# A hybrid decoder layer on one core: the order of the first gathered blocks, and of ScalarE's copies behind them

## The chip, the core and the metric

The kernel runs on one core of one Trainium2 chip. The metric is the time of one execution on the device, in microseconds (us). A core has five engines that matter here, each with its own queue of instructions, worked in order: TensorE (PE in the profile, with its weight loads as PEld), VectorE (DVE), ScalarE (ACT), GpSimd (POOL) and SyncE (SP). They meet through semaphores. TensorE writes its results into PSUM, which has eight banks; VectorE and ScalarE copy them out into SBUF.

## The reference, cut to what matters

One decoder layer over 256 tokens of width 2048: two groups of attention heads, an output projection and a layer norm; then PEER, a retrieval of single-neuron experts; then a gated embedding. All three norms are over alpha times the residual plus the new part. The change lies in PEER:

```python
q = (xt @ wq).reshape(t, PEER_HEADS, PEER_QDIM)
sa = jnp.einsum('thc,nc->thn', qa, sub_keys[0])
sb = jnp.einsum('thc,nc->thn', qb, sub_keys[1])
va, ia = lax.top_k(sa, PEER_TOPK)
vb, ib = lax.top_k(sb, PEER_TOPK)
top, sel = lax.top_k(cand, PEER_TOPK)            # cand: all sums va + vb
eidx = jnp.take_along_axis(cidx, sel, axis=-1)   # cidx = ia * 128 + ib
gates = jax.nn.softmax(top, axis=-1)
act = jax.nn.gelu(jnp.einsum('thed,td->the', u[eidx], xb))
out = jnp.einsum('the,thed->td', gates * act, v[eidx])
```

Each token picks, in each of 8 heads, 16 of 16384 experts. An expert has a row of u and a row of v, 2048 numbers each. A token's dot product with the u row goes through gelu, is weighted by the gate, and multiplies the v row.

## The kernel before, in words

**Stages.** In order of time: the attention projections and heads, the output projection and first norm, the PEER queries and scores with the top-16 searches on VectorE, the sorting of the experts, the u blocks, the v blocks, the second norm, the gated embedding and the third norm.

**Which experts are gathered.** The last 224 tokens form seven groups of 32 ("units" 1 to 7; the first 32 tokens go another way, row by row, through `sparse_work`). `flags` counts with products of one-hot matrices which experts each unit uses. `classes` sorts the experts by the set of units that use them: one unit (singles), two (pairs), three that lie on a "line", four that form a "quad", and the rest. There are 42 such classes and the rest; each is a 128 x 128 matrix of flags in `I`. `classes` is a generator: its first half makes the seven quads (K4 to KR), its second, at the second `next(sorting)`, everything else (K1 to K4). A class has a fixed number of slots, and 128 slots of the same units make a block. There are 101 blocks; `U_ORDER` is the order in which they are worked: the first six quad blocks, then quads, lines, strips (pairs) and singles mixed, then the rest mixed with the remaining singles. A block is "wide" where its units lie at even steps, so that one product takes all of them; the first nine quad blocks are all wide, with four units each.

**From flags to row numbers.** For a class, `offsets(k0, k1)` (L1029) counts the flags of each column with one product a class, copies the counts (`cs`), sums them over the columns before with one more product, and copies that (`off`). `running(k0, n, tag, on_act)` (L1046) makes running counts of up to four classes, two 128-wide products a class, and copies them out on ScalarE or VectorE. `list_marks`, `list_rows` and `list_index` then find for three blocks at a time the row number of each slot (`idx`). `lists(i1)` is a generator over these up to block i1, and `list_work` runs `lists(6)`, then the ten `running` calls over all classes but quads and the rest, then `lists` for the others, then more. A step of it is run either directly (`run(listing, 1)`), or by `fetch_u` when a block's row numbers are still missing, or by `pace`: this takes a number of microseconds and runs, for each of them, 0.9 steps of the side work that is next (the gates, the lists, then the placing of the gates in `W`), and a share of the gathers for the first 32 tokens.

**A u block.** `fetch_u` (L1437) issues the indirect gather of 128 rows of u on GpSimd into one of five slots. `turn(i, c)` (L1444), for c from 0 to 3, transposes 128 x 512 of block i with four TensorE products (L1451) into one of three PSUM banks with tag T, and copies that to `uT` on ScalarE (L1453). `u_products` (L1455) makes the dot products: for a wide block sixteen products that have `uT` as their weights (L1459; the trace shows each as two instructions), with a `pace` after every second one; for the others products of 32 tokens at a time, that lay the units beside one another in the bank (L1474). Results go to one of two PSUM banks with tag U; `running` uses these tags, too. `u_out` (L1502) brings the result into the order of `W`: for a wide block with a gelu from the bank (L1539 or L1523), for another block first with transposes or products on TensorE from `part`, a copy of the bank (L1658), and then with a gelu. Where the gate already stands in `W`, the gelu goes to `acts`, and `weigh` multiplies it into `W` on VectorE later.

**The order around the change** is written out by hand: `keep` keeps each engine's instructions in the order of the program. Before the loop over the blocks stand five gathers, the four turns of block 0, the second half of the sorting, `offsets(0, K4)`, one list step and two steps of the gates. In the loop, block i + 1 is turned ahead of the products of block i. In the first pass, a list step follows the first two turns of block 1 in the place of a pace. Behind the products of block i stands on ScalarE either the gelu of a wide block, or the copy `part` of another one, whose `u_out` comes after the last turn of the next pass.

**The v blocks** follow: 101 gathers of 128 rows of v and products with `W` into seven banks (L1686). Up to thirteen rows' slots can be filled ahead; the first four gathers start once the placing is done.

Of the kernel before, what the change touches and what calls it, by code (L numbers as in the profile page):

```python
# [10 lines left out]
F32 = mybir.dt.float32  # L11
# [9 lines left out]
P = 128  # L21
# [52 lines left out]
K4 = K3 + len(LINES)  # L74
KR = K4 + len(QUADS)
NK = KR + 1
# [84 lines left out]
START, BLOCKS, NC = _blocks()  # L161


def _mix(*lists):

    todo = [(j + 0.5) / len(x) for x in lists for j in range(len(x))]
    flat = [b for x in lists for b in x]
    return [flat[i] for i in sorted(range(len(flat)), key=lambda i: todo[i])]
# [1 line left out]

NEARLY = 14
SINGLES = [BLOCKS["single"][6 * g + k] for k in range(6) for g in range(NG)]
U_ORDER = (BLOCKS["quad"][:6] + _mix(BLOCKS["quad"][6:], BLOCKS["line"], BLOCKS["strip"],
                                     SINGLES[:NEARLY])
           + _mix(BLOCKS["rest"], SINGLES[NEARLY:]))
NB = len(U_ORDER)
# [117 lines left out]
def build(tc, a, out):  # L294
    nc = tc.nc
# [490 lines left out]
    keep = tc.keep_in_program_order  # L786
# [242 lines left out]
    def offsets(k0, k1):  # L1029

        ps = pbank(pu, "ps_off", "G", 2)
        for k in range(k0, k1):
            keep(nc.tensor.matmul(ps[:, k:k + 1], I[:, k, 2:], ones16[:, :1], start=True,
                                  stop=True))
        keep(nc.vector.tensor_copy(cs[:, k0:k1], ps[:, k0:k1]))
        keep(nc.tensor.matmul(ps[:, 64:64 + k1 - k0], ahead, cs[:, k0:k1], start=True, stop=True))
        if k1 == NK:
            keep(nc.tensor.matmul(ps[:, 128:129], ones16, cs[:, KR:NK], start=True, stop=True))
        keep(nc.vector.tensor_copy(off[:, k0:k1], ps[:, 64:64 + k1 - k0]))
        if k1 == NK:  # L1040
            keep(nc.vector.tensor_scalar(total, ps[:, 128:129], -float(CAPR), 0.0, op0=ALU.add,
                                         op1=ALU.max))
            keep(nc.vector.tensor_scalar(okc, ps[:, 128:129], float(CAPR), 1.0 / GSCALE,
                                         op0=ALU.is_le, op1=ALU.mult))
# [44 lines left out]
    def lists(i1):  # L1089

        nonlocal listed
        made = []
        for i0 in range(listed, i1, 3):
            n = min(3, i1 - i0)
            es = [list_marks(i) for i in range(i0, i0 + n)]
            made.append((i0, n, list_rows(i0, es)))
            yield
            if len(made) > 1:
                i, m, ps = made.pop(0)
                list_index(i, m, ps)  # L1100
                listed = i + m
                yield
        while made:
            i, m, ps = made.pop(0)
            list_index(i, m, ps)
            listed = i + m
            yield
# [33 lines left out]

    def list_work():

        yield from lists(6)
        for i, (k0, n) in enumerate([x for r in ((K3, K4), (K2, K3), (K1, K2))
                                     for x in spread(*r)]):
            running(k0, n, "TU"[i % 2], i % 3 < 2)
            if i % 3 == 2:
                yield
        yield from lists(UPOS[id(BLOCKS["rest"][0])])  # L1150
        for lo, hi in ((K1, K2), (K2, K3), (K3, K4), (K4, KR)):
            for k0, n in spread(lo, hi):
                yield from places_of(k0, n)
        yield
        keep(nc.vector.scalar_tensor_tensor(I[:, KR, 2:], posf, 0.0, some, op0=ALU.is_equal,
                                            op1=ALU.mult))
        offsets(KR, NK)
        yield
        running(KR, 1, "G", True)
        yield  # L1160
        yield from places_of(KR, 1)
        pu32 = lp.tile([P, P], U32, name="pu32")
        keep(nc.vector.tensor_copy(pu32, posf))
        keep(nc.vector.tensor_scalar(pu32, pu32, 13, 0x38000000, op0=ALU.logical_shift_left,
                                     op1=ALU.bitwise_or))
        keep(nc.vector.tensor_copy(map16, pu32.bitcast(F32)))
        yield
        yield from lists(NB)
# [189 lines left out]
    def run(work, n):  # L1358

        for _ in range(n):  # L1360
            if next(work, "end") == "end":
                return True
        return False
# [52 lines left out]
    pools.close("hotp")  # L1416
    sorting = classes(flp, cnt, I, some)
    next(sorting)
    offsets(K4, KR)
    for i, (k0, n) in enumerate(spread(K4, KR)):  # L1420
        running(k0, n, "TU"[i], i == 0)

    listing, gating, sparse, placing = list_work(), gates(), sparse_work(), None
# [20 lines left out]
    def turn(i, c):  # L1444
        if i >= NB:
            return
        if not c:
            turned[i] = ulp.tile([P, D], F32, name="uT", tag="uT", bufs=2)
        ps = pbank(pu, "ps_T", "T", 3)
        for j in range(4):  # L1450
            keep(nc.tensor.transpose(ps[:, j * P:(j + 1) * P],  # L1451
                                     rows[i][:, (4 * c + j) * P:(4 * c + j + 1) * P], ident))
        keep(nc.scalar.copy(turned[i][:, c * 512:(c + 1) * 512], ps))  # L1453
# [46 lines left out]
    late = []  # L1500
# [113 lines left out]
    def weigh(n):  # L1614
        while len(late) > n:
            dst, x = late.pop(0)
            keep(nc.vector.tensor_tensor(dst, dst, x, op=ALU.mult))
# [3 lines left out]
    def pace(us):  # L1621
        side(us)
        gathers(us * grate)
# [1 line left out]
    for _ in range(WF):  # L1625
        fetch_u()
    ulp = pools.open("ulp", "left", bufs=1)
    for c in range(4):
        turn(0, c)
    next(sorting)  # L1630
    offsets(0, K4)
    pools.close("flp")
    run(listing, 1)
    run(gating, 2)
    pending = None
    for i, block in enumerate(U_ORDER):
        grate = GRATES[i >= UPOS[id(BLOCKS["rest"][0])]]
        fetch_u()
        old = len(late)
        for c in range(4):  # L1640
            turn(i + 1, c)
            if c == 3 and pending:
                u_out(*pending)
                pending = None
            if i or c > 1:
                pace(block.quarter)
            else:
                run(listing, 1)
            if c == 1:
                weigh(len(late) - old)  # L1650
        ps = pbank(pu, "ps_u", "U", 2)
        u_products(block, ps, turned.pop(i))
        if block.wide:
            u_out(block, ps)
        else:
            n = P * len(block.windows)
            part = ulp.tile([P, 512], F32, name="part", tag="part", bufs=2)
            keep(nc.scalar.copy(part[:, :n], ps[:, :n]))  # L1658
            pending = block, part
        held = max(min(NB - 2 - i, WF), 0)  # L1660
        if i >= NB - LEAD - NVX - 1 and places_done:
            fetch_v(0)
    if pending:
        u_out(*pending)
    weigh(0)
    assert places_done
    pools.close("ulp", "pu")
# [321 lines left out]
    ps = ln2_T(0, 0, 2)  # L1989
# [17 lines left out]
    ps = ln2_T(1, 0, 4)  # L2007
# [8 lines left out]
    ps = ln2_T(1, 4, 4)  # L2016
# [191 lines left out]
```

## Time and profile before

| what | value |
|---|---|
| time, median of 3 runs | 1519.4 us (1517.67 to 1522.47) |
| the profiled execution's own time | 1515.78 us |
| its span, first to last instruction | 1513.7 us |
| mean granted TensorE clock | 0.97 |
| TensorE busy | 1405.3 us, 93% of the span |
| VectorE, ScalarE, GpSimd busy | 892.4, 634.0 and 430.9 us |
| DMA, mean over the span | 266 GB/s, 402.79 MB |
| first transposes of a u block | at 599.0 us |
| last transposes of a u block | at 1138.9 us |

Lines are those of the kernel before. In a group or a timeline row, `ps_T<-ident,uf` means that `ps_T` is written from `ident` and `uf`, `x16` that sixteen such instructions are taken together, and the part in brackets or behind the last bar is idle time of the engine before them with what ended it. TensorE's products are pipelined and their ends are modelled. A clock of 1.00 is full speed.

### The profile page before, as it was taken

The page shows a single profiled execution, that of the slowest core. Times are in us where ns is not written, and L with a number is a line of the kernel's source. Part 1 is how long each engine was busy: PE and PEld are TensorE (multiplying, and loading weights), DVE is VectorE, ACT ScalarE, POOL GpSimd, SP SyncE. Part 2 cuts the span into 40 slices and gives each one's busy share as a digit, 9 for nine tenths or more (in the row PEclk, how much of TensorE's full clock was granted, in tenths as well). Part 3 has the DMA queues.
Part 4 walks back from the last instruction along what each step waited for, and adds up shares of the span by engine and source line. Part 5 has one row for each costly group of instructions (what it writes and reads, how often), then busy time and mean ns, then how long its engine had stood idle before and what let it go on. Part 6 is the DMA issues. An engine that isn't in the chain of part 4 may idle for free.

```text
span 1513.7 us, 32441 instructions
## 1 busy us (share of the span) xinstructions
PE 1405.3 (93%) x13184; PEld 1092.3 (72%) x13184; DVE 892.4 (59%) x2487; ACT 634.0 (42%) x1311; POOL 430.9 (28%) x386
## 2 busy tenths in 40 slices
PE   9999999999999945999999899988999999995898
PEld 7888888887888834997888888888885333331686
DVE  5455568976559996679756676778532000005767
ACT  5578547875411154444544454444451000003632
POOL 0033213310120021243443343442554444421000
PEclk9999999999999966999999999999999999997899
DMA  8655665558544102788899888899999999999471
GB/s 305 198 167 167 204 201 153 149 161 317 185 153 150 30 30 110 289 297 322 301 353 344 297 325 309 320 394 362 376 383 396 420 418 418 414 385 347 170 267 56
DMA packets 74587, 402.79 MB, mean 266 GB/s; under 512 B 10836, under 2 KB 12916, under 8 KB 36436
## 3 DMA queue, kind: packets, MB, share of 16 engines
q0 software_dynamic: 39280, 272.11, 46.2%
q1 hardware_dynamic: 33424, 125.41, 24.8%
q10 hardware_dynamic: 1728, 3.15, 0.6%
q8 instruction: 104, 1.70, 0.4%
q14 instruction: 51, 0.42, 0.1%
HBM read 404.97 MB, written 4.45 MB: 270 GB/s over the span
## 4 chain that ended last, share of the span: by engine, by line
PE 69%; DMA 10%; issue 8%; DVE 5%; ACT 4%; POOL 3%; POOLq 0%; another core or an unknown queue 0%; ACTq 0%; DVEq 0%
PE ps_T L1451 12%; PE ps_u L1474 8%; PE ps_qk L333 8%; PE ps_q L345 7%; PE ps_u L1459 7%; PE ps_qk L335 4%; DMA vf<-v_rows,idx 4%; DMA vx<-v_rows,idx 3%; PE ps_v L352 2%; PE ps_v L353 2%; PE ps_v L354 2%; PE ps_gate L352 2%; PE ps_gate L353 2%; PE ps_gate L354 2%; PE ps_mix L353 1%
## 5 line engine op out<-in xcount | busy, mean ns | idle before, releaser
L236 DVE TENSOR_TENSOR wl<-wf,wh 128x1024 fp32r<-128x1024 f32 (+1 forms) x167 | 193.0, 1170 | 102.9 <-ACT wh L235 101.6
L1451 PE MATMUL ps_T<-ident,uf 128*128 128x128 f32 x1616 | 220.7, 279 | 26.2 <-ACT uT L1453 17.7
L1453 ACT COPY uT<-ps_T 128x512 f32<-128x512 f32 x404 | 213.6, 598 | 36.5 <-PE ps_T L1451 32.6
L1426 POOL DMA_INDIRECT uf<-u_rows,idx x101 | 132.2, 1309 | 316.2 <-PE ps_T L1451 136.1
L1451 PEld LDWEIGHTS ps_T<-ident,uf 128*128 128x128 f32 x1616 | 176.1, 142 | 50.7 <-ACT uT L1453 25.3
L235 ACT CAST wh<-wf 128x1024 fp32r<-128x1024 f32 (+1 forms) x167 | 155.0, 945 | 114.2 <-PE ps_v L354 30.3
L333 PE MATMUL ps_qk<-X,wh 128*128 128x512 f32 x512 | 185.2, 401 | 0.0
L335 PE MATMUL ps_qk<-X,wl 128*128 128x256 f32 x512 | 145.7, 285 | 0.0
L1474 PE MATMUL ps_u<-uT,XF 128*32 128x128 f32 x3904 | 136.8, 275 | 7.4 <-issue 7.2
L1459 PE MATMUL ps_u<-XF,uT 128*128 128x128 f32 (+2 forms) x832 | 132.5, 311 | 0.0
L1733 DVE BATCH_NORM_STATS2 st<-ps_v 128x6 f32<-128x512 f32 x8 | 5.6, 700 | 213.6 <-PE ps_v L1769 160.5
L1686 PE MATMUL ps_v<-vf,W 128*32 128x512 f32 x936 | 112.0, 612 | 18.2 <-DMA vf<-v_rows,idx 18.2
L1474 PEld LDWEIGHTS ps_u<-uT,XF 128*32 128x32 f32 x3904 | 105.5, 109 | 25.1 <-issue 20.8
L1459 PEld LDWEIGHTS ps_u<-XF,uT 128*128 128x128 f32 x832 | 119.9, 192 | 0.3
L345 PE MATMUL ps_q<-XF,wf 128*128 128x256 f32 x512 | 113.5, 379 | 0.0
L333 PEld LDWEIGHTS ps_qk<-X,wh 128*128 128x128 f32 x512 | 96.4, 188 | 22.0 <-issue 1.0
L1201 DVE SCALAR_TENSOR_TENSOR junk<-io,ibF,ps_find 128x128 f16<-128x128 f16 x224 | 64.5, 344 | 75.7 <-PE ps_find L1193 65.0
L345 PEld LDWEIGHTS ps_q<-XF,wf 128*128 128x128 f32 x512 | 95.9, 190 | 12.3
L1331 DVE SCALAR_TENSOR_TENSOR y<-gb,ew,y 128x2048 f32<-128x2048 f32 x31 | 72.8, 2348 | 47.3 <-DMA gb<-v_rows,eig 47.3
L1686 PEld LDWEIGHTS ps_v<-vf,W 128*32 128x32 f32 x936 | 32.7, 111 | 91.1 <-issue 68.9
L335 PEld LDWEIGHTS ps_qk<-X,wl 128*128 128x128 f32 x512 | 96.3, 188 | 2.5 <-issue 1.3
L1658 ACT COPY part<-ps_u 128x128 f32<-128x128 f32 (+1 forms) x75 | 22.1, 295 | 144.0 <-PE ps_u L1474 85.9
(357 smaller groups left out, 2512.6 us busy)
## 6 DMA issues: line engine op xcount, KB each, us to landing
wf<-w_qk SPq DMA_DIRECT2D x64, 512.0 KB, 3.6
wf<-w_out SPq DMA_DIRECT2D x32, 512.0 KB, 3.6
wf<-peer_wq SPq DMA_DIRECT2D x16, 1024.0 KB, 5.2
wf<-ple_gate SPq DMA_DIRECT2D x16, 1024.0 KB, 9.8
wf<-w_v SPq DMA_DIRECT2D x16, 512.0 KB, 4.1
wf<-w_sv SPq DMA_DIRECT2D x15, 512.0 KB, 6.0
iarow<-s_iar SPq DMA_DIRECT2D x14, 512.0 KB, 8.8
x<-x SPq DMA_DIRECT2D x2, 1024.0 KB, 5.8
```

Of the source, the lines that this page charges most:

```text
L235: self.order(nc.scalar.copy(wh, src))
L236: self.order(nc.vector.tensor_tensor(wl, src, wh.bitcast(F32), op=ALU.subtract))
L333: nc.tensor.matmul(ps, wh[:, j * P:(j + 1) * P], xt[:, dt, :], start=dt == 0, stop=False)
L335: nc.tensor.matmul(ps[:, :T], wl[:, j * P:(j + 1) * P], xt[:, dt, :T], start=False, stop=dt == ND - 1)
L345: nc.tensor.matmul(ps[:, :T - t0], wf[:, dt * P:(dt + 1) * P], xt[:, dt, t0:], start=dt == 0, stop=dt == ND - 1)
L353: order(nc.tensor.matmul(ps, hi, wl, start=False, stop=False))
L1426: keep(nc.gpsimd.indirect_dma_start(out=dst, out_offset=None, in_=src, in_offset=bass.IndirectOffsetOnAxis(ap=idx[:, col:col + 1], axis=0) ...
L1451: keep(nc.tensor.transpose(ps[:, j * P:(j + 1) * P], rows[i][:, (4 * c + j) * P:(4 * c + j + 1) * P], ident))
L1453: keep(nc.scalar.copy(turned[i][:, c * 512:(c + 1) * 512], ps))
L1459: keep(nc.tensor.matmul(ps[:, :n], uT[:, d * P:(d + 1) * P], groups_of(d, *block.wide), start=d == 0, stop=d == ND - 1))
L1474: keep(nc.tensor.matmul(ps[32 * q:32 * q + 32, w * P:(w + 1) * P], XF[:, d, t0:t0 + 32], uT[:, d * P:(d + 1) * P], start=first and not w, ...
L1686: keep(nc.tensor.matmul(ps[32 * j:32 * j + 32], w, vf[:, j * 512:(j + 1) * 512], start=False, stop=last))
```

## The change

Four things are changed. The first nine quad blocks, not six, stand at the front of `U_ORDER`, and `list_work` lists them before its running counts. `offsets` becomes a generator that pauses between its counts and the rest; for the classes of the second half of the sorting, the sorting and the counts are put ahead of the first turn of block 0, and the rest of `offsets` between the first turn and the other three. The three direct list steps are gone. In the first pass, the products of block 0 come first and block 1 is turned behind them, with a pace after each of its four turns. And in all passes, the bank of block i - 1 is taken care of between the turns of block i + 1: the copy `part` of a block that is not wide behind the first turn, and `u_out`, with the gelu of a wide block too, behind the fourth.

```diff
+NFIRST = 9
+U_ORDER = (BLOCKS["quad"][:NFIRST] + _mix(BLOCKS["quad"][NFIRST:], BLOCKS["line"], BLOCKS["strip"],
...
         keep(nc.vector.tensor_copy(cs[:, k0:k1], ps[:, k0:k1]))
+        yield
...
-        yield from lists(6)
+        yield from lists(NFIRST)
...
-        offsets(KR, NK)
+        list(offsets(KR, NK))
...
-    offsets(K4, KR)
+    list(offsets(K4, KR))
...
-    for c in range(4):
+    next(sorting)
+    placed = offsets(0, K4)
+    next(placed)
+    turn(0, 0)
+    list(placed)
+    for c in range(1, 4):
         turn(0, c)
-    next(sorting)
-    offsets(0, K4)
     pools.close("flp")
-    run(listing, 1)
     run(gating, 2)
-    pending = None
+    behind = []
+
+    def parts_out(block, ps):
+        if block.wide:
+            return block, ps
+        n = P * len(block.windows)
+        part = ulp.tile([P, 512], F32, name="part", tag="part", bufs=2)
+        keep(nc.scalar.copy(part[:, :n], ps[:, :n]))
+        return block, part
+
+    def next_turned(i):
+        old = len(late)
+        for c in range(4):
+            turn(i + 1, c)
+            if c == 0 and behind:
+                behind[0] = parts_out(*behind[0])
+            if c == 3 and behind:
+                u_out(*behind.pop())
+            pace(U_ORDER[i].quarter)
+            if c == 1:
+                weigh(len(late) - old)
+
     for i, block in enumerate(U_ORDER):
         grate = GRATES[i >= UPOS[id(BLOCKS["rest"][0])]]
         fetch_u()
-        old = len(late)
-        for c in range(4):
-            turn(i + 1, c)
-            if c == 3 and pending:
-                u_out(*pending)
-                pending = None
-            if i or c > 1:
-                pace(block.quarter)
-            else:
-                run(listing, 1)
-            if c == 1:
-                weigh(len(late) - old)
+        if i:
+            next_turned(i)
         ps = pbank(pu, "ps_u", "U", 2)
         u_products(block, ps, turned.pop(i))
-        if block.wide:
-            u_out(block, ps)
-        else:
-            n = P * len(block.windows)
-            part = ulp.tile([P, 512], F32, name="part", tag="part", bufs=2)
-            keep(nc.scalar.copy(part[:, :n], ps[:, :n]))
-            pending = block, part
+        if not i:
+            next_turned(i)
+        behind.append((block, ps))
...
-    if pending:
-        u_out(*pending)
+    u_out(*parts_out(*behind.pop()))
```

More of the change, by code (lines that the diff above doesn't have):

```diff
@@ L172 @@
 SINGLES = [BLOCKS["single"][6 * g + k] for k in range(6) for g in range(NG)]
-U_ORDER = (BLOCKS["quad"][:6] + _mix(BLOCKS["quad"][6:], BLOCKS["line"], BLOCKS["strip"],
+NFIRST = 9
+U_ORDER = (BLOCKS["quad"][:NFIRST] + _mix(BLOCKS["quad"][NFIRST:], BLOCKS["line"], BLOCKS["strip"],
                                      SINGLES[:NEARLY])
```

## The prediction, made before the changed kernel was run

> **What bounds the kernel now.** I read the page's slices first, then TensorE's timeline where the changed code begins, then the clock there, then the waits of the long stage behind it.
>
> ```profile
> span 1513.7 us, 32441 instructions
> ...
> PE   9999999999999945999999899988999999995898
> ```
>
> TensorE is busy nearly everywhere. The deep dip (slices 14 and 15, 530 to 605 us) is the passage from the scores to the u rows. The change starts at the end of that dip. TensorE there (start, length, idle time before and what ended it):
>
> ```profile
> 599.00 3.57 PE L1451 MATMUL ps_T<-ident,uf 128*128 128x128 f32 x16 [7.23 <-DMA uf<-u_rows,idx]
> 602.40 1.02 PE L1033 MATMUL ps_off<-ones,I 128*128 128x1 f16 x35
> 604.51 0.18 PE L1036 MATMUL ps_off<-cs,ahead 128*128 128x35 f16 x1 [1.09 <-DVE cs L1035]
> ...
> 618.45 0.66 PE L1451 MATMUL ps_T<-ident,uf 128*128 128x128 f32 x4 [0.68 <-ACT uT L1453]
> 618.95 3.29 PE L1459 MATMUL ps_u<-XF,uT 128*128 128x128 f32 x28
> ...
> 622.74 1.99 PE L1451 MATMUL ps_T<-ident,uf 128*128 128x128 f32 x16
> ```
>
> TensorE waits 7.23 us for the first gathered rows, turns them, does the 35 column counts, waits 1.09 us for their copy, and stands 0.68 us at 618.45. At 618.95 begin the second block's products; I use that as the landmark, since everything before it is the same work in both kernels. The granted clock in three stretches (columns: length; busy time of PE, PEld, DVE, ACT, POOL; clock; DMA share; GB/s):
>
> ```profile
> 598.90:602.30 3.40, 3.30 (x16) 3.30 (x17) 0.00 (x0) 1.61 (x3) 0.79 (x1) 0.50 0.99 414
> 602.30:605.70 3.40, 2.31 (x59) 2.23 (x58) 0.39 (x2) 1.25 (x4) 0.99 (x1) 1.00 1.01 426
> 605.70:609.10 3.40, 3.40 (x32) 3.34 (x30) 1.02 (x2) 2.35 (x6) 0.00 (x0) 0.51 1.01 426
> ```
>
> It rises to 1.00 after a busy stretch of 3.4 us and falls back to 0.5 after the stretch that holds the counts and the 1.09 us wait.
>
> From 640 to 1140 us TensorE's stage is the u blocks. Its waits there (total, times, longest), the largest kind:
>
> ```profile
> PE ps_T L1451 <- ACT uT L1453: 17.0, 22, 2.4
> ```
>
> Behind that the v rows run gapless on TensorE:
>
> ```profile
> L1686 PE MATMUL ps_v<-vf,W 128*32 128x512 f32 x891 | 101.5, 592 | 0.0
> L1686 PE MATMUL ps_v<-vx,W 128*32 128x512 f32 x662 | 77.1, 592 | 0.5 <-issue 0.5
> ```
>
> **The change part by part.** *Counts into the gather's shadow.* The sorting's second half, the 35 counts and the copy now come ahead of the second to fourth transpose groups. VectorE before:
>
> ```profile
> 590.37 1.06 DVE L1063 TENSOR_SCALAR mark<-io,off 128x128 f16<-128x128 f16 x6
> ...
> 597.45 0.19 DVE L1009 TENSOR_SCALAR some<-wh 128x128 f16<-128x128 f16 x1
> 604.26 0.20 DVE L1035 CAST cs<-ps_off 128x35 f16<-128x35 f32 x1 [6.63 <-PE ps_off L1033]
> ```
>
> With nine blocks listed ahead instead of six, one list step of three marks more stands before the third index: 3 x 1.06/6 = 0.53 us. Sorting then ends near 597.45 + 0.53 = 598.0, the counts near 599.1, about 0.15 us after the rows land at 599.0. So of the counts' 1.02 us some 0.85 is gained, and the 1.09 us wait goes whole, as the copy (0.20 us) lies under the first transpose group (3.57/4 = 0.9 us). Without the shadow, if sorting came 2 us later, the counts would cost what they do now. Bounds of both together: 0.9 to 2.1; I take 1.94.
>
> *Clock.* With the counts gone from 602.3 to 605.7 and dense products there instead, the stretch at 0.51 should run at 1.00: half of 3.4 us, 1.7. Bounds 0 and 1.7. The row shows sixteen transposes alone (x16, then 1.00) lifting the clock. The Trainium skill, "TensorE: Matmul & The Clock Gate", section "Part 4: PE-mode transpose", says that transposes do not count as busy; by that, 598.9 to 602.3 would not have lifted it, the gain would be 0 and the sum 4.1. The row decides against it. The same page's section "Part 1: The HAM clock gate" has the window free-running, which would make this gain a matter of chance; that is a rival below.
>
> *Table load.* The first gelu stands today between the products and the copies that the next transposes need:
>
> ```profile
> 616.35 1.28 ACT L1539 ACT_TABLE_LOAD   x1 [3.39 <-PE ps_u L1459]
> 617.65 0.28 ACT L1539 ACTIVATE W<-ps_u 128x128 f32<-128x128 f32 x1
> 617.82 2.05 ACT L1453 COPY uT<-ps_T 128x512 f32<-128x512 f32 x4
> ```
>
> Behind the third block's copies, its 1.28 + 0.28 us lie under the second block's products (over 3.3 us): the 0.68 us stall goes. Uncovered it would cost those 1.56 us at most. The Trainium skill, "ScalarE: Activation LUTs", section "What ACT_TABLE_LOAD costs", adds a drain of about 1.38 us to each switch; here the gelu starts 0.02 us after the load, so the trace does not show it, and by the page the sum would not change, as even 2.9 us fit.
>
> *One bank held.* The first block's products keep one of the two U banks until that late gelu, so the running counts with tag U (five of ten) share the other one: each waits for the copy of the one before. The work up to the landmark (35 matrices, two products each):
>
> ```profile
> L1451 PE MATMUL ps_T<-ident,uf 128*128 128x128 f32 x48 | 8.6, 335 | 7.9 <-DMA uf<-u_rows,idx 7.2 <-ACT uT L1453 0.7
> L1052 PE MATMUL ps_run<-after,I 128*128 128x128 f16 x35 | 5.5, 251 | 0.0
> L1051 PE MATMUL ps_run<-upto,I 128*128 128x128 f16 x35 | 5.5, 251 | 0.0
> ...
> L1072 PE MATMUL ps_rows<-run,mark 128*128 128x129 f16 (+1 forms) x11 | 1.1, 225 | 0.0
> ```
> ```profile
> L1057 DVE CAST run<-ps_run 128x512 f16<-128x512 f32 (+1 forms) x4 | 2.6, 658 | 5.5 <-PE ps_run L1052 5.5
> ```
> ```profile
> L1055 ACT CAST run<-ps_run 128x512 f16<-128x512 f32 (+2 forms) x7 | 3.4, 514 | 2.3 <-PE ps_run L1052 2.0
> ```
>
> No row shows a bank conflict. Lower bound 0; upper bound, a copy (0.66) behind two queued ScalarE copies (2.05/4 = 0.51 each, above) four times, near 6.7. Only one pair stands in the same step (the fourth and sixth count), with one T count between them; I take 0.5, near the lower bound.
>
> *Turning the second block later.* Its sixteen transposes (1.99 us), four ScalarE copies and the 70 running products change places with 32 products; none is added. What TensorE issues before the landmark stays the same save about eight of the eleven list products (L1072, 1.1 us), which come later: borrowed, not won, so left out. On GpSimd's queue stand the gathers; the seventh:
>
> ```profile
> 614.52 0.99 POOL L1426 DMA_INDIRECT uf<-u_rows,idx  x1 [10.69 <-PE ps_rows L1072]
> ```
>
> The seventh block's gather waits for its index today and for the second block's slot then, near 613 (the landmark less this gain, 615, less one turn of 2 us): no later. Of the 48 transposes to the landmark only the first waits for a gather (7.2 us), and the rows are five blocks ahead, so neither SyncE nor GpSimd sets anything. The three direct list steps become paced ones, leaving the lists about one step behind: nothing, while it does not delay the v rows' first gathers.
>
> *ScalarE's order in the u blocks.* A late case (ScalarE, then TensorE):
>
> ```profile
> 995.74 0.27 ACT L1658 COPY part<-ps_u 128x128 f32<-128x128 f32 x1 [2.67 <-PE ps_T L1451]
> 995.90 2.06 ACT L1453 COPY uT<-ps_T 128x512 f32<-128x512 f32 x4
> ```
> ```profile
> 993.87 1.53 PE L1451 MATMUL ps_T<-ident,uf 128*128 128x128 f32 x12
> 996.55 0.65 PE L1451 MATMUL ps_T<-ident,uf 128*128 128x128 f32 x4 [1.15 <-ACT uT L1453]
> ```
>
> The fourth transpose group needs the first group's copy. The part copy ahead of it delays that by only 995.90 - 995.74 = 0.16 us; the other 1.9 us, from 993.87, where the products had been issued, to 995.74, are TensorE's signal coming late, which the order on ScalarE does not touch. So the 17.0 us shrink by at most 22 x 0.16 = 3.5, and by 0 if the late signal sets the pace anyway; I take 2.0. For wide blocks the copies do not wait for the gelus today:
>
> ```profile
> 628.56 0.34 ACT L1539 ACTIVATE W<-ps_u 128x64 f32<-128x64 f32 x2 [3.07 <-PE ps_u L1459]
> 629.05 2.29 ACT L1453 COPY uT<-ps_T 128x512 f32<-128x512 f32 x4 [0.15 <-PE ps_T L1451]
> ```
>
> The copy is released by its transposes, 0.15 us idle after the gelus: moving these gains 0. Three wide quads go to the front, three fewer among the small blocks; up to three more late cases of 17.0/22 = 0.77 us each, or none; I take 0.
>
> **Sum.** 1.94 + 1.70 + 0.68 - 0.50 + 2.00 = 5.8 us. The profiled execution took 1515.78 us (span 1513.7 and 2.1 around it), so 1510.0 for it; it stands 3.6 below the median of the three runs, 1519.4, and the same gain on the median gives 1513.6. The gain is at its full size at the end only because the v rows follow TensorE without a gap.
>
> **Rivals.** *Only the start pays* (20 in 100): the late signals set the pace, the 2.0 fall away; gain 3.8, 1515.6. For it: 1.9 of each 2.0 us of a late case are signal. Against: the fourth group is released by the copy itself.
>
> *The clock's window* (10): it falls elsewhere, the 1.7 fall away; gain 4.1, 1515.3. For it: no row ties the edges of the stretches to an instruction. Against: each of the three stretches is told by the activity in the one before.
>
> *The v rows take it back* (12): the gathers, not TensorE, pace the v rows.
>
> ```profile
> 1160.00:1180.00 20.00, 20.00 (x192) 6.05 (x188) 0.00 (x0) 0.00 (x0) 7.63 (x10) 1.00 1.01 419
> ```
>
> A DMA share of 1.01 speaks for it; the missing gaps at the v products speak against. If the rows come no earlier than now, the gain is 0 to 1: 1519.
>
> *The bank, slower* (10): the shared U bank costs its upper bound. Place: the second block's turn. Gaps of 1.7 us would also bring the half-clock stretch back and a second one with it: 1.94 - 1.7 + 0.68 - 6.7 + 2.0 = -3.8, so 1523.2. It decides once the bank costs 6.3 us with the full clock, or 2.9 with those two stretches. For it: tag U is on every second count. Against: the counts are spread over paces with transposes between.
>
> **Chances.** The forecast has 48 in 100, with an own range of 1511 to 1516. Under about 0.3% (4.6 us on 1519.4) no change can be told. Faster by more: 0.42 of the forecast's 0.48, a fifth of the first rival, a third of the second, 0.49 in all. Within: the rest of these and nearly all of the third, 0.40. Slower: the bank and mishaps of its kind, 0.11. The range runs from every term at its best (2.1 + 1.7 + 0.68 + 3.5 = 8.0, and 1.4 for the spread of the runs: 1510) to about half of the bank rival's loss (1521).
>
> **What would show it.** Right: the counts end before or just at the first transposes; no wait of about 1 us for the copy of the counts; full clock from the first products on; the second block's products start near 615 instead of 618.95; the table load lies under them; the waits of transposes for ScalarE fall by some 2 us with as many events, the part copy standing behind the first copy. Wrong: idle time before running counts released by their copies; half clock after 606; the 17.0 unchanged or larger; gaps released by DMA at the v products. The forecast fails if the start's gain is not there at the first v product.

## The result and the profile after

The changed kernel takes 1511.3 us (median of six, 1508.0 to 1513.8) against 1519.7 us (median of six, 1517.7 to 1523.9) for the kernel before: 8.4 us less, a ratio of 0.9942 with a 95% interval of 0.9922 to 0.9962. Run once more among the first four experiments, it was 1509.8 against 1519.3, ratio 0.9922 (0.9898 to 0.9946). The forecast was 1513.6, a gain of 5.8. The profiled execution took 1511.78 us, 4.0 less than the profiled one of before: the traces below can show only these 4.0.

TensorE from the counts to the landmark, the start of the second block's products (timeline of the changed kernel: start, length, operation, idle time before it and what ended it):

```profile
598.65 1.09 PE L1034 MATMUL ps_off<-ones,I 128*128 128x1 f16 x35 [4.78 <-DVE I L985]
599.60 1.09 PE L1453 MATMUL ps_T<-ident,uf 128*128 128x128 f32 x4
600.78 0.19 PE L1038 MATMUL ps_off<-cs,ahead 128*128 128x35 f16 x1
600.80 2.80 PE L1453 MATMUL ps_T<-ident,uf 128*128 128x128 f32 x12
603.40 2.60 PE L1461 MATMUL ps_u<-XF,uT 128*128 128x128 f32 x20
...
615.42 0.61 PE L1461 MATMUL ps_u<-XF,uT 128*128 128x128 f32 x4
615.96 0.59 PE L1074 MATMUL ps_rows<-run,mark 128*64 128x129 f16 x5
```

The counts stand ahead of the first transposes and nobody waits for their copy. The landmark is at 615.42 instead of 618.95, which is 3.5 us earlier. The counts of the quads, ahead of all that was changed, begin at 587.57 before and at 588.15 in the changed kernel; from there to the landmark it is 4.1 us less. ScalarE there (timeline of the changed kernel):

```profile
616.36 0.59 ACT L1455 COPY uT<-ps_T 128x512 f32<-128x512 f32 x1 [0.16 <-PE ps_T L1453]
616.96 1.28 ACT L1541 ACT_TABLE_LOAD   x1
618.26 0.28 ACT L1541 ACTIVATE W<-ps_u 128x128 f32<-128x128 f32 x1
```

The table load lies under the second block's products, behind the copies, as forecast. The stretch from the first transposes to the landmark, of before and then of the changed kernel (windows: length; busy time and count of PE, PEld, DVE, ACT, POOL; granted clock; DMA share; GB/s):

```profile
599.00:618.95 19.95, 18.18 (x198) 17.52 (x198) 7.91 (x35) 10.66 (x21) 4.24 (x5) 0.83 0.71 282
```
```profile
599.60:615.42 15.82, 15.42 (x160) 14.84 (x158) 5.70 (x26) 8.89 (x18) 3.01 (x4) 0.87 0.78 313
```

Length times clock is the stretch at full clock: 19.95 x 0.83 = 16.6 us before, 15.82 x 0.87 = 13.8 after. So of the 4.1 us that the stretch is shorter, 2.8 are work and waits that left it, and 1.3 are clock. Not all of the 2.8 is won. The groups of the same stretch of the changed kernel (busy, mean ns, idle before):

```profile
L1054 PE MATMUL ps_run<-after,I 128*128 128x128 f16 x35 | 4.4, 219 | 0.0
L1053 PE MATMUL ps_run<-upto,I 128*128 128x128 f16 x35 | 4.4, 219 | 0.3 <-ACT run L1057 0.3
...
L1074 PE MATMUL ps_rows<-run,mark 128*128 128x129 f16 x3 | 0.3, 220 | 0.0
```

Three list products (0.3 us) stand where eleven stood (1.1 us): 0.8 us come later. And the shared U bank makes the running counts wait 0.3 us, once.

Farther on, the waits of the transposes from 640 to 1150 us, of before and then of the changed kernel (groups by line):

```profile
L1451 PE MATMUL ps_T<-ident,uf 128*128 128x128 f32 x1520 | 206.0, 278 | 18.3 <-ACT uT L1453 17.0 <-ACT part L1658 1.1
```
```profile
L1453 PE MATMUL ps_T<-ident,uf 128*128 128x128 f32 x1504 | 203.7, 279 | 19.5 <-ACT uT L1455 19.4
```

These did not fall. The profile has a wait besides that the first profile of before doesn't have, for VectorE's flags of the last class (timeline), and behind it a stretch of 6.83 us at half clock (windows):

```profile
713.62 0.19 PE L1034 MATMUL ps_off<-ones,I 128*128 128x1 f16 x1 [2.59 <-DVE I L1157]
```
```profile
713.04:719.87 6.83, 6.00 (x78) 5.26 (x79) 0.97 (x7) 0.91 (x3) 1.17 (x1) 0.50 0.55 180
```

The half clock does not have to follow: the second profile of the same kernel (after_again, below) has the same wait, 2.58 us, and a clock of 1.00 over the same stretch.

The prediction said that its forecast fails if the start's gain is not there at the first v product. That product starts at 1153.7 before and at 1151.9 in the changed kernel: 1.8 us of the landmark's 3.5 are left. And the v rows do not run gapless to their end. The prediction read 0.0 in a view that ends at 1372; behind that the last v products wait for gathers, in before and then in the changed kernel (groups of the whole span):

```profile
L1686 PE MATMUL ps_v<-vf,W 128*32 128x512 f32 x936 | 112.0, 612 | 18.2 <-DMA vf<-v_rows,idx 18.2
```
```profile
L1698 PE MATMUL ps_v<-vf,W 128*32 128x512 f32 x936 | 111.8, 612 | 14.9 <-DMA vf<-v_rows,idx 14.9
```

With 3.3 us less of these waits the last v product starts 4.8 us earlier (1397.0 instead of 1401.8), and the span is 3.7 us shorter. No run tests why these waits became shorter.

So the start came out nearly as forecast and the u blocks did not. The two profiles gained less than the forecast 5.8 us, the medians more.

### The profile page after: what moved, and what is told of

Same layout as the page of the kernel before. It is cut to its first block, busy times and chain, and to the rows that moved or that the text cites. A ratio compares the mean times of both kernels' runs of the same rounds, so it can differ in the third digit from the quotient of the medians.

```text
span 1510.0 us, 32409 instructions
## 1 busy us (share of the span) xinstructions
PE 1405.9 (93%) x13184; PEld 1093.0 (72%) x13184; DVE 892.2 (59%) x2491; ACT 625.8 (41%) x1316; POOL 432.1 (29%) x386
## 4 chain that ended last, share of the span: by engine, by line
PE 70%; DMA 11%; issue 8%; DVE 5%; ACT 3%; POOL 3%; POOLq 0%; ACTq 0%; DVEq 0%
PE ps_T L1453 12%; PE ps_qk L334 8%; PE ps_u L1461 8%; PE ps_u L1476 8%; PE ps_q L346 7%; DMA vf<-v_rows,idx 5%; PE ps_qk L336 4%; PE ps_v L353 2%; PE ps_v L354 2%; PE ps_v L355 2%; PE ps_gate L353 2%; PE ps_gate L355 2%; PE ps_gate L354 2%; PE ps_mix L354 1%; PE ps_mix L355 1%
## 5 line engine op out<-in xcount | busy, mean ns | idle before, releaser
L1455 ACT COPY uT<-ps_T 128x512 f32<-128x512 f32 x404 | 219.0, 602 | 296.5 <-PE ps_T L1453 286.0
L1453 PE MATMUL ps_T<-ident,uf 128*128 128x128 f32 x1616 | 220.0, 280 | 19.5 <-ACT uT L1455 19.4
L1698 PE MATMUL ps_v<-vx,W 128*32 128x512 f32 x672 | 78.6, 592 | 0.3 <-issue 0.3
```

What stands on the lines that cost most here:

```text
L1453: keep(nc.tensor.transpose(ps[:, j * P:(j + 1) * P], rows[i][:, (4 * c + j) * P:(4 * c + j + 1) * P], ident))
L1698: keep(nc.tensor.matmul(ps[32 * j:32 * j + 32], w, vf[:, j * 512:(j + 1) * 512], start=False, stop=last))
```

## The experiments

Each set of four ran on one chip beside the kernel before. On the first and second chip that took 1519.3 and 1519.9 us (medians), on the third 1483.2; each kernel is held against its own. The ratios and the differences of medians part by up to 3 us, so single sizes below are good to a few us only.

### The parts by themselves

**after_again** is the changed kernel, unaltered.

> The changed kernel once more, beside the three below on the same chip, so that the parts can be added up. Every theory: 7 to 10 us under the kernel before, as in the first comparison (median 1511.3 against 1519.7).

Measured: 1509.8 us, ratio 0.9922 (0.9898 to 0.9946), 9.6 us less by the medians.

**start_alone**, in the changed kernel:

```
 def next_turned(i):
...
-    if c == 0 and behind:
-        behind[0] = parts_out(*behind[0])
...
-behind.append((block, ps))
+if block.wide and i:
+    u_out(block, ps)
+else:
+    behind.append(parts_out(block, ps))
```

> The changed start alone (counts split over the gather's shadow, second block turned behind the first one's products, nine wide quads ahead, first gelu behind the third block's copies); from the second block on ScalarE's order is that of the kernel before: wide gelus and part copies right behind their products. Theory 1, the prediction's terms with their sizes: 1.94 + 1.70 + 0.68 - 0.50 = 3.8 us gained, and some 4.6 of the 8.4 measured must then be ScalarE's order. Theory 2, the start is worth the whole gain (the trace of after shows the bank's wait at 0.3 instead of 0.5, and the landmark 3.5 to 4.1 us earlier, the rest being clock and fewer late signals): 7 to 9 us gained. Landmark near 615.4 in both.

Measured: 1515.0 us, ratio 0.9957 (0.9942 to 0.9973): 4.4 us less than before by the medians, 6.5 by the ratio (4.1 to 8.8), and 5.2 more than the changed kernel. By the medians that is theory 1 (3.8), by the ratio it is nearer to theory 2 (7 to 9), so the run doesn't decide between them. The landmark is at 615.70.

**order_alone**, in the kernel before, with the change's `parts_out` and `behind`; the second block is still turned ahead of the first one's products, and six quads stand ahead:

```
-if c == 3 and pending:
-    u_out(*pending)
-    pending = None
+if c == 0 and behind:
+    behind[0] = parts_out(*behind[0])
+if c == 3 and behind:
+    u_out(*behind.pop())
...
-if block.wide:
-    u_out(block, ps)
...
+behind.append((block, ps))
```

> The kernel before with ScalarE's new order alone (wide gelus behind the next block's copies, part copies behind the next block's first copy); start, turns and the order of blocks as before. Theory 1: 2.0 us for the order and 0.68 for the table load, which now lies behind the third block's copies: 2.7 us gained, up to 4.6 if the order carries the rest of the measured gain. Theory 2: only the 0.68, within 1 us of before. The waits of transposes for ScalarE are 17.0 us in the kernel before; theory 1 has them below 15, theory 2 at 17 to 19.

Measured: 1514.4 us, ratio 0.9970 (0.9948 to 0.9992): 5.0 us less, which is theory 1 by the time. 0.9957 x 0.9970 = 0.9927 beside 0.9922 for the whole change: the two parts add up within their intervals.

**nine_alone**, in the kernel before:

```
-U_ORDER = (BLOCKS["quad"][:6] + _mix(BLOCKS["quad"][6:], ...
+U_ORDER = (BLOCKS["quad"][:9] + _mix(BLOCKS["quad"][9:], ...
...
-    yield from lists(6)
+    yield from lists(9)
```

> The kernel before with nine instead of six wide quads ahead in the order of blocks (and nine blocks listed before the first transposes), nothing else. Prediction: 0 (loss of up to 3 x 0.77 us if three more small blocks in a row end late, or the like as a gain if they end earlier). If the order of blocks carries a hidden part of the 8.4 us, it shows here as over 2 us.

Measured: 1525.5 us, ratio 1.0024 (1.0005 to 1.0044): 6.2 us more by the medians, 3.6 by the ratio (0.8 to 6.7). The edit that I costed at nothing is a loss when it stands alone. Its stretch to the landmark, then that of start_alone (windows):

```profile
599.25:623.26 24.01, 21.30 (x194) 20.01 (x195) 7.19 (x32) 10.83 (x21) 3.94 (x5) 0.69 0.62 245
```
```profile
600.02:615.70 15.68, 15.32 (x159) 14.74 (x157) 5.64 (x26) 8.89 (x18) 3.00 (x4) 0.87 0.77 311
```

At full clock nine_alone's stretch is 24.01 x 0.69 = 16.6 us, as in before: in this profile, of an execution of 1529.19 us, it lost 4.1 us more to the clock, and to nothing else. The last index of the longer list takes the first step between the turns, and the running counts come one step later. The profile shows half clock from the first transposes to 612.85, but doesn't show that this step is the cause. With the new start (13.6 at full clock) that loss is not there. So the same nine quads cost 4 to 6 us with the old start, and the new start gains 10.5 us on top of them (1525.5 - 1515.0); of that the two profiles show 5.3 us as clock: 24.01 - 16.6 = 7.4 us lost against 15.68 - 13.6 = 2.1.

Transposes' waits from 640 to 1150 us (groups by line), of nine_alone, start_alone and order_alone:

```profile
L1451 PE MATMUL ps_T<-ident,uf 128*128 128x128 f32 x1531 | 206.5, 278 | 27.3 <-ACT uT L1453 25.7 <-issue 1.0
```
```profile
L1453 PE MATMUL ps_T<-ident,uf 128*128 128x128 f32 x1507 | 203.8, 278 | 25.3 <-ACT uT L1455 24.5 <-issue 0.7
```
```profile
L1451 PE MATMUL ps_T<-ident,uf 128*128 128x128 f32 x1520 | 205.8, 278 | 19.7 <-ACT uT L1453 18.0 <-issue 1.6
```

Nine quads ahead with the old order on ScalarE raise these waits from 17.0 to about 25 us; the new order brings them back to 19.4 (19.2 in after_again). With nine ahead that fits the time: start_alone to after_again is 5.2 us by the medians and 24.5 - 19.2 = 5.3 us of waits. With six ahead it does not: order_alone gained 5.0 us by the medians, while its waits (18.0) did not fall below 15, as theory 1 had them, and its profiled execution took 1515.82 us, as long as that of before (1515.78). Where those 5.0 us lie I can't show.

### Is nine needed, and what in ScalarE's order pays

**after_six**, in the changed kernel:

```
-NFIRST = 9
+NFIRST = 6
```

> The changed kernel with six instead of nine wide quads ahead. Theory 1 (the parts add up: nine ahead cost 5 to 6 us in the kernel before whatever the start is): 4 to 6 us under the changed kernel, about 1505. Theory 2 (nine ahead cost so much only because the three extra list steps pushed the running counts of the old start out of the stretch at full clock, 2.8 us of it by the first products): within 2 us of the changed kernel, about 1510.

Measured: 1511.7 us against 1519.9, ratio 0.9948 (0.9931 to 0.9964), beside 0.9942 and 0.9922 for the changed kernel on other chips: theory 2 by the time. In the changed kernel six or nine quads ahead make no difference that these intervals show; whether the new start or the new order on ScalarE makes them harmless is not separated, as no run has six ahead with the new start and the old order. The transposes wait 16.5 us here.

**parts_only** and **wide_only**, each in the changed kernel:

```
 # parts_only
-behind.append((block, ps))
+if block.wide and i:
+    u_out(block, ps)
+else:
+    behind.append((block, ps))
 # wide_only
-    if c == 0 and behind:
-        behind[0] = parts_out(*behind[0])
...
-behind.append((block, ps))
+behind.append(parts_out(block, ps))
```

> The changed kernel, but wide blocks' gelus stand right behind their products again (save the first block's); part copies stay behind the next block's first copy. The prediction: moving wide gelus gains 0, so this takes the changed kernel's time, 1510, and the whole of ScalarE's 5 us against the changed start alone. Rival: the wide gelus carry it, and this takes the time of the changed start alone, 1515.

Measured: 1515.3 us, ratio 0.9966 (0.9953 to 0.9979), near start_alone's (0.9957): the part copies' place alone gains nothing that the intervals show, as the rival had it.

> The changed kernel, but part copies stand right behind their products again; wide gelus stay behind the next block's copies. The prediction (0.16 us for each of the late small blocks, and 0 for the gelus): the time of the changed start alone, 1515. Rival: 1510, as the changed kernel.

Measured: 1512.8 us, ratio 0.9949 (0.9931 to 0.9968), between the two values expected, with both inside the interval. The waits of both, in this order (groups by line, 640 to 1150 us):

```profile
L1453 PE MATMUL ps_T<-ident,uf 128*128 128x128 f32 x1505 | 203.0, 278 | 25.2 <-ACT uT L1455 24.3 <-issue 0.7
```
```profile
L1453 PE MATMUL ps_T<-ident,uf 128*128 128x128 f32 x1504 | 203.0, 278 | 20.9 <-ACT uT L1455 20.6
```

From start_alone's 24.5 the wide gelus' place takes 3.9 us, and the part copies' place, once the gelus are moved, 1.2 more (to 19.4); by itself it takes 0.2. That is the reverse of my costing. It rests on one profile of each, from two chips, and the times go the same way. The same two small blocks in start_alone, then in wide_only (timeline of TensorE):

```profile
973.44 0.66 PE L1453 MATMUL ps_T<-ident,uf 128*128 128x128 f32 x4 [1.45 <-ACT uT L1455]
...
978.13 0.66 PE L1453 MATMUL ps_T<-ident,uf 128*128 128x128 f32 x4 [1.43 <-ACT uT L1455]
```
```profile
971.82 0.66 PE L1453 MATMUL ps_T<-ident,uf 128*128 128x128 f32 x4 [0.37 <-ACT uT L1455]
...
973.56 2.04 PE L1453 MATMUL ps_T<-ident,uf 128*128 128x128 f32 x16
```

No gelu of a wide block stands next to these waits. What changed is at which small blocks ScalarE's copies start late, and through what the gelus act on that stays open.

### The clock, the split counts, the first gelu

**warm**, in the changed kernel, `warm(40)` ahead of the counts of the last classes and `warm(44)` ahead of those of the others:

```
+def warm(n):
+    ps = pbank(pu, "ps_warm", "T", 3)
+    for _ in range(n):
+        keep(nc.tensor.matmul(ps[:, :P], ahead, upto, start=True, stop=True))
```

> The changed kernel with 40 idle matmuls (128x128, result unread) in TensorE's 4.3 us of idle time before the counts of the last classes and 44 in the 4.8 us before the counts of the others, which computes more than the reference needs and changes no output. Theory 1 (the clock follows the activity of the window before): full clock from about 590, the 5.2 us from the counts to the first products' start shrink to about 2.6, landmark 2 to 3 us earlier, time 1.5 to 3 us under the changed kernel. Theory 2 (the edges of the half-clock stretches are not set by activity): half clock to about 604 as before, time within 1 us of the changed kernel.

Measured: 1513.8 us, ratio 0.9952 (0.9936 to 0.9968). Its clock (windows):

```profile
576.50:586.70 10.20, 8.60 (x76) 7.95 (x76) 8.71 (x19) 4.27 (x12) 0.00 (x0) 0.50 0.01 2
586.70:593.50 6.80, 4.08 (x54) 3.05 (x53) 5.35 (x29) 0.58 (x1) 0.79 (x1) 1.00 0.00 0
593.50:597.00 3.50, 3.50 (x38) 3.50 (x35) 3.40 (x11) 0.00 (x0) 2.66 (x3) 0.51 0.71 192
597.00:600.40 3.40, 1.81 (x43) 1.49 (x42) 1.15 (x6) 0.00 (x0) 2.03 (x2) 1.00 0.97 364
600.40:603.80 3.40, 3.40 (x18) 3.34 (x17) 1.63 (x10) 1.93 (x4) 0.00 (x0) 0.50 1.02 422
600.08:615.41 15.33, 15.01 (x156) 14.63 (x156) 5.71 (x26) 8.88 (x18) 2.63 (x3) 0.89 0.72 293
```

Theory 1 holds for the clock: a busy stretch is followed by full clock, and one with gaps (4.08 of 6.80, 1.81 of 3.40) by half. In the changed kernel the clock is 0.50 from 581.9 to 602.3. But the last gaps, behind the idle matmuls, put half clock on the window of the transposes again, and the stretch to the landmark is 15.33 us, hardly shorter than 15.50 and 15.82 in the two profiles without them. No gain in time shows.

**counts_behind**, in the changed kernel:

```
+for c in range(4):
+    turn(0, c)
 next(sorting)
-placed = offsets(0, K4)
-next(placed)
-turn(0, 0)
-list(placed)
-for c in range(1, 4):
-    turn(0, c)
+list(offsets(0, K4))
```

> The changed kernel, but the counts stand behind the first block's transposes in one piece, as before the change; the second block is still turned behind the first one's products. The prediction's term for the split alone: 1.94 us, so landmark near 617.4 instead of 615.4 and 1512 to 1513. Rival (what the split mostly buys is the clock: 2 us of extra idle time ahead of the products lengthen the half-clock stretch by one window): landmark near 619, time 1514 or more.

Measured, on the third chip: 1482.0 us against 1483.2, ratio 0.9993 (0.9983 to 1.0004). That is 1.9 us more than gelu_first, next, which has the split counts; the two intervals overlap.

**gelu_first**, in the changed kernel:

```
 if not i:
+    u_out(block, ps)
     next_turned(i)
-behind.append((block, ps))
+else:
+    behind.append((block, ps))
```

> The changed kernel, but the first block's gelu, with its table load, stands right behind its products, ahead of the second block's copies. The prediction's two terms: the bank's wait (0.3 us in the changed kernel's trace) goes and the table load's 0.68 us stall (up to 1.56) comes back: landmark 0.2 to 1.3 us later, time within 1.5 us of the changed kernel. Rival: the load delays the copies that release the transposes' banks by its full 1.28 us plus a half-clock window, landmark 2 to 3 us later.

Measured, on the third chip: 1480.1 us, ratio 0.9983 (0.9971 to 0.9996). The stretches of counts_behind and gelu_first (windows), and a wait in the latter (groups by line):

```profile
600.01:616.78 16.77, 16.16 (x189) 15.72 (x190) 5.70 (x26) 9.21 (x19) 3.05 (x4) 0.88 0.74 293
```
```profile
600.64:616.19 15.55, 15.19 (x160) 14.70 (x158) 5.68 (x26) 10.43 (x21) 2.98 (x4) 0.89 0.78 314
```
```profile
L1053 PE MATMUL ps_run<-upto,I 128*128 128x128 f16 x35 | 4.4, 219 | 0.4 <-ACT W L1541 0.4
```

The split shortens the stretch by 16.77 - 15.55 = 1.2 us on this chip, with the clock alike in both (0.88, 0.89). The wait for the counts' copy is 0.3 us here, in counts_behind as in before_again. In the three profiles of the old start on the other chips (before, order_alone, nine_alone) it is 1.05 to 1.09, so there the split should be worth 0.8 us more, about 2.0; that is an estimate from these waits. The gelu's place changes nothing: the stretch is 15.55 us here and 15.59 in after_steps, which has the changed kernel's start and ran on the same chip. The running counts wait 0.4 us for the gelu's bank in place of 0.3 for a copy's, and the table load stalls no transposes.

### A wait taken away, and before once more

**after_steps**, in the changed kernel:

```
 keep(nc.vector.scalar_tensor_tensor(I[:, KR, 2:], posf, 0.0, some, ...
+yield
+yield
 list(offsets(KR, NK))
```

> The changed kernel with two more steps between VectorE's flags of the last class and their counts on TensorE (the counts that made TensorE wait 2.58 us at 713 in the changed kernel's profile, behind a 2.28 us VectorE operation of the sparse rows). Theory 1 (the wait is on the path to the end): it goes, the half-clock stretch that follows it in some profiles goes, and the time falls by 2.5 to 4 us, to about 1507. Theory 2 (the wait is taken back before the rest blocks or by late signals): within 1 us of the changed kernel, 1510.

Measured, on the third chip: 1479.5 us, ratio 0.9977 (0.9967 to 0.9988), 0.6 us under gelu_first, which I take as the changed kernel there, since the changed kernel itself did not run on this chip; so no time of gelu_first can be held against the changed kernel's. TensorE in gelu_first, then in after_steps, then VectorE in after_steps (timelines):

```profile
713.37 0.18 PE L1034 MATMUL ps_off<-ones,I 128*128 128x1 f16 x1 [3.69 <-DVE I L1157]
...
765.05 0.40 PE L1195 MATMUL ps_find<-map,oht 128*128 128x128 f16 x4 [1.37 <-DVE oht L1186]
```
```profile
760.79 0.61 PE L1197 MATMUL ps_find<-map,oht 128*128 128x128 f16 x4 [4.36 <-DVE oht L1188]
```
```profile
759.98 0.75 DVE L1188 TENSOR_SCALAR oht<-iarow,lin 128x2048 f16<-128x2048 f16 x1 [8.65 <-DMA iarow<-s_iar]
```

The 3.69 us wait is gone, and another has grown from 1.37 to 4.36 us, since VectorE's step ahead of it waits for a load. 3.0 of 3.7 us are given back; theory 2.

**before_again** is the kernel before.

> The kernel before once more, for a second profile: its first profiled execution took 1515.78 us, under all later timings (1516.5 to 1526.8, median 1519.3). Theory 1: a usual execution of 1518 to 1522 us loses its 3 to 6 us among the u blocks, in more waits of transposes for ScalarE's copies than the 17.0 us of the first profile (20 or more), which would be the room in which the new order of ScalarE gained 5 us. Theory 2: the waits stay at 17, and the difference is in half-clock stretches.

Measured, on the third chip: 1483.1 us. Its stretch to the landmark (windows), its transposes and its small blocks' products from 640 to 1150 us (groups by line; the products of the first profile of before are put between), and the small block whose case the prediction showed (timeline of all engines):

```profile
600.07:618.25 18.18, 16.98 (x198) 16.07 (x199) 8.01 (x35) 10.46 (x21) 4.31 (x5) 0.90 0.79 314
```
```profile
L1451 PE MATMUL ps_T<-ident,uf 128*128 128x128 f32 x1520 | 202.6, 278 | 2.1 <-DMA uf<-u_rows,idx 1.8 <-issue 0.3
```
```profile
L1474 PE MATMUL ps_u<-uT,XF 128*32 128x128 f32 x3904 | 136.8, 275 | 7.4 <-issue 7.2
```
```profile
L1474 PE MATMUL ps_u<-uT,XF 128*32 128x128 f32 x3904 | 123.1, 275 | 1.8 <-issue 1.8
```
```profile
967.60 2.04 PE L1451 MATMUL ps_T<-ident,uf 128*128 128x128 f32 x16
...
967.73 0.27 ACT L1658 COPY part<-ps_u 128x128 f32<-128x128 f32 x1 [2.02 <-PE ps_u L1474]
...
968.35 2.05 ACT L1453 COPY uT<-ps_T 128x512 f32<-128x512 f32 x4 [0.34 <-PE ps_T L1451]
```

Neither theory: from 640 us on not one transpose waits for ScalarE. The part copy starts 0.13 us after the transposes began; in the profile that the prediction read it was 995.74 - 993.87 = 1.87 us. The last transposes start at 1101.4 instead of 1138.9 us, so the 32.7 us between the two profiles arise in the u blocks: these waits are 17.0 us there, and the small blocks' products 19.3, as they occupy TensorE 13.7 us less and leave it idle 5.6 us less. So the late starts, and with them all that ScalarE's order can gain through the 17.0 us, go with the chip; each chip ran only one set, so no more than that is shown. The wait for VectorE's flags that the changed kernel has at 713 is in this profile of before too (2.9 us). And the second half-clock stretch of the start is not there: 18.18 x 0.90 = 16.4 us at full clock, 1.8 lost instead of 3.4.

## Why the prediction was right and wrong

**The start: right in sum, by other shares.** 3.82 us were forecast. The stretch to the landmark got 4.1 us shorter, less the 0.8 us of list products that come later, which the prediction had set aside as borrowed: 3.3. The terms without the clock, 1.94 + 0.68 - 0.50 = 2.12, measured 2.8 - 0.8 = 2.0. Of these the counts' 1.94 is 1.2 on the third chip (counts_behind), where the wait for their copy is 0.3 us; on the others, where it is the 1.09 us that I read, 1.94 agrees with the estimate of 2.0, but no run tested it there. The bank's wait is 0.3 us instead of 0.50. The stall of 0.68 us is gone, but not for the reason that I gave: gelu_first has the load ahead of the copies again and no stall, so turning the second block later takes it away, wherever the gelu stands.

**The clock: a term of chance, booked as sure.** 1.70 was forecast and 1.3 is what the first two profiles show. The rival that I gave 10 in 100 said 0. On the first chip of the experiments, order_alone's old start loses 4.2 us (19.21 us at 0.78) and after_again's new one 1.9 (15.50 us at 0.88), so 2.3; on the third chip before_again loses 1.8 and gelu_first 1.7, so 0.1. The stretch that I took as saved is missing in before_again (clock 0.90 against 0.83). Whether that is chance, or comes from the shorter wait for the counts' copy there, isn't shown. The Trainium skill, "TensorE: Matmul & The Clock Gate", section "Part 1: The HAM clock gate", calls the activity window free-running and its penalty variable from run to run; the two profiles of the changed kernel agree, with clocks of 0.50 and 1.00 behind the same wait at 713.

**Nine quads ahead: wrong.** "None is added; I take 0" held for the instructions. But with the old start this costs 6.2 us by the medians (3.6 by the ratio); its profile loses 4.1 us to the clock at the start, and the waits of the transposes rise by 8.7. Inside the change it costs nothing that I could measure (after_six). The prediction's 0 is right for the whole, but not for the reason it gave: a loss stands there against a gain that grew with it.

**ScalarE's order: right to pay, wrong in size and place.** 2.00 us were forecast, all by the part copies, and 0 for the wide gelus because their copies are released by transposes. Measured: 5.2 us for both (start_alone to after_again, with 5.3 us less of waits), about nothing for the part copies alone (0.9966 beside start_alone's 0.9957), 1 to 3 us for the wide gelus alone (0.9949 by the ratio; by the medians 7.1 under before instead of 4.4). The intervals of these ratios overlap; the waits (24.3 and 20.6 us) go the same way. The step that failed is "moving these gains 0": it looked only at the copy next to the gelu. And the sign of being right that I named, 17.0 us falling by 2, did not come, but a sign of being wrong, the 17.0 larger: with nine ahead the new order of blocks raises that sum first, to 24.5, and with six ahead (order_alone, after_six) it stays at 16.5 to 18.0 in either order. So the 2.00 were taken from waits that this edit does not shorten in the kernel before.

**The wait at 713** was not in the forecast at all. The profiles shown have it at 2.59 and 3.69 us. On the third chip before has it too, so it is not the change's alone. Taking it away gave little back.

**The path to the end.** "The gain is at its full size at the end only because the v rows follow TensorE without a gap" was read from a view that stops at 1372. Behind it TensorE waits 18.2 us for gathers in before and 14.4 to 16.5 in the profiles with the new start on the chips where before takes 1519 us (on the third chip 20.5 in before_again, 19.7 in gelu_first). So 2 to 4 us of what the traces gain there lie in a wait that the prediction held to be nothing, and nothing was run on it.

**Luck.** A gain of 8.4 us beside a forecast of 5.8 has the right direction, and 1511.3 us lies at the fast edge of 1511 to 1516. That is in part luck: two terms that were put at 0, the nine quads and the wide gelus, were not 0 and work against each other, and on the third chip the change, as gelu_first, is worth some 3 us only.

**The rivals.** "Only the start pays" (1515.6) describes start_alone's median (1515.0) well, but not the change. On the third chip, where no transposes wait for ScalarE, gelu_first's 3.1 us (2.5 by the ratio) are near that rival's 3.8. "The bank, slower" fell: 0.3 us instead of 6.7. "The v rows take it back" (1519) fell by the time itself, though its sign, gaps released by DMA at the v products, is there in both kernels.

**Open.** The profiled execution of before, 1515.78, lies under all 29 later timings beside the first set (1516.5 to 1526.8), so the two profiles show 4.0 us where the medians show 8.4. No trace of a usual execution of before on such a chip exists, and what makes it 3.5 us longer isn't shown. Why ScalarE's copies start late on two chips and not on the third isn't known either, nor what the change gains there exactly. The ends of TensorE's products are modelled, so the traces can't tell a late signal from products that end late.

## What to carry to other kernels

Weigh a stretch by length times granted clock before adding up its terms: it separates the work that left (2.8 us here) from the clock that may or may not come back. When an edit changes an order, cost it with the old and the new surroundings: nine quads ahead cost 4 to 6 us in the one and nothing measurable in the other. Read a stage to its end before calling it gapless. A wait for a signal that comes late with no work behind it may be the chip's and not the kernel's: profile on a second chip before building on it.

## What was unexpected of the hardware

The same program took 1519 us on two chips and 1483 on a third; the 17.0 us for which its transposes waited for ScalarE are gone there, and its small blocks' products take TensorE 13.7 us less, though every instruction is the same. ScalarE's part copy, 1.9 us behind the transposes at one block of the first profile, is 0.13 us behind them at that block on the third chip. And idle matmuls did lift the clock (1.00 from 586.7 to 593.5, where the changed kernel has 0.50) but could not hold it across gaps of 1.6 us in all in a window of 3.4.
